# One ring of four PSUM banks, and a retention branch whose value products run a block late, in a two-layer hybrid encoder on one core

## Chip, cores and metric

The kernel runs on one core of a Trainium2 chip. The metric is the device time of one execution in microseconds (us). Three runs of the kernel before took 2946.37, 2948.24 and 2952.17 us, a median of 2948.24 us.

## What is computed

A trunk of two layers over 528 tokens (16 learned ones and 512 of the input) of width 1024, in float32. Each layer mixes tokens in two parallel branches, merges them, and adds a feed-forward block. Cut to its core:

```
proj = rms_norm(h) @ w_in
(qkv, z, a, b, q_b, k_b, v_b, g_b, gate_a, gate_b) = split(proj)
# branch a: 8 heads of 128, both directions, 64-token chunks
q, k, v = silu(short_conv(qkv)); q, k l2-normalised
o_a = gated_delta(q, k, v) + flip(gated_delta(flip(q, k, v)))
y_a = (rms(o_a) * gain * silu(z)) @ w_up_a
# branch b: 4 heads, keys of 256, values of 512
o_b = sum_m gamma^|n-m| (rope(q_n) . rope(k_m)) v_m     # both directions
y_b = (rms(o_b) * silu(g_b)) @ w_up_b
h = h + (sigmoid(gate_a) * y_a + sigmoid(gate_b) * y_b) @ w_out
h = h + (silu(x @ w_gate) * (x @ w_up)) @ w_ffn_out      # x = rms_norm(h)
```

After two layers there is a last norm, and the 512 input tokens are written out.

## The kernel before

**Projections.** Activations lie transposed, as eight tiles of 128 features by 528 tokens, each split into a rounded part and a remainder (`xh`, `xl`). A weight block of 1024 x 128 arrives by DMA as `wraw`; ACT rounds it to `whi` and DVE takes the remainder `wlo` (`split`, lines 178 to 180). `project` then issues three matmuls for each of eight blocks and each half of the tokens (264 columns, or 512 in one piece in the second layer, which drops the learned tokens from most results): 48 or 24 matmuls to an output tile `mmps`, which ACT or DVE reads out of PSUM (`consume`).

**PSUM.** Its eight banks are three rings of [128 x 512] tiles: `pmm` (2 banks) holds the `mmps` of every projection, `pmx` (2, through `pt`) everything that retention, the norms, the sums and the output turns make, and `pmc` (4, through `ct`) the delta rule and the first units behind a norm. A matmul into a ring's next tile waits until the tile that held the bank has been read.

**Mixing.** Four groups of two delta-rule heads run one after the other. `gdn_begin` makes a group's q, k, v, and `gdn_chain` runs its chain: products (`kk`, `kq`), a solve of 32 x 32 blocks on DVE (`st`, `w0`), which goes through DRAM at its start (`nd`, back as `w0`) and its end (`xd`, back as `qc`), the levels that join the blocks (`gdn_levels`: PE `lvy`, `lvt`, `lvq`, `l64`, `l64b`, with DVE and ACT between them), and a scan of five steps (`gdn_scan`: `ks`, `yy`, `sn`, `oo`). It has little PE work and many hand-overs. So `weave` runs it against a filler: each generator yields numbers, its estimated work, and `weave` takes from the filler `NB` = 86 for each `NA` = 71 of the chain. The filler is `filling()`: retention of heads 0 to 2, z gates and merge gates. What is left when the four chains end, and retention of head 3, follows. A scheduler in the framework makes the final order on each engine out of the program's order and priorities.

**Retention** (`retention`, lines 929 to 1017). A mask `strip` is loaded and exponentiated on ACT; q and k are projected, copied by ACT (`rp`, line 946) and rotated on DVE (`rot`). Then, for five chunks, scores `rs` = k.q on PE, times the mask on DVE (`pr`), split into `prh` and `prl`. Then, for four value blocks `dv`, in this order: value projection, ACT copy `rvc` (line 987), turn on PE (`rvt`, `rvm`, lines 995 and 998), split `rv`, gate projection (`rg`), and the weighted sum `rpv` = scores x values. Its yields are 1.8 a chunk, 5.4 a projection and 4.5 a value block.

**After mixing** come the up-projections (`load_a`, `load_b`, results `mrg` and `yb`), the output projection and the feed-forward block. In the last one `done` squares and scales each output half tile and `laid` turns it on PE (`ops`, line 1290) to token order.

Of the kernel before, what the change touches and what calls it, by code (L numbers as in the profile page):

```python
# [48 lines left out]
UB = 6  # L49
TB = 4  # L50

# [46 lines left out]
def trunk(ctx: ExitStack, tc: tile.TileContext, x, meta, norm_mix, w_in, conv_w, a_log, dt_bias, gdn_norm,  # L98
# [6 lines left out]
    tp = ctx.enter_context(tc.tile_pool(name="tp", bufs=TB))  # L105
    pmm = ctx.enter_context(tc.tile_pool(name="pmm", bufs=2, space=PSUM))
    pmx = ctx.enter_context(tc.tile_pool(name="pmx", bufs=2, space=PSUM))
    pmc = ctx.enter_context(tc.tile_pool(name="pmc", bufs=4, space=PSUM))
# [25 lines left out]
    def pt(name="px"):  # L134
        return pmx.tile([P, 512], F32, name=name, tag="mx")

# [165 lines left out]
    with tc.tile_pool(name="ip", bufs=1) as ip:  # L302
# [23 lines left out]
        def turned(i):  # L326
            return pmm.tile([P, 512], F32, name="lay", tag="mm") if i % 2 else pt("lay")

# [72 lines left out]
def layer(tc, nc, env, l, xn, gd):  # L401
# [14 lines left out]
    def acc(tiles):  # L416
        return lambda k: tiles[k]

    def project(src, c0, nt, xs, halves, consume, kts=(8,)):

        xh, xl = xs
        for t in range(nt):
            pss = [pmm.tile([P, 512], F32, name="mmps", tag="mm") for _ in halves]
            k0 = 0
            for j, kt in enumerate(kts):
                w = weights(src[k0 * P:(k0 + kt) * P], c0 + t * P, kt)
                for (n0, n), ps in zip(halves, pss):
                    mm3(ps, w, acc(xh), acc(xl), kt, n0, n, first=j == 0, last=j == len(kts) - 1, k0=k0)
                k0 += kt
            for (n0, n), ps in zip(halves, pss):  # L430
                consume(t, n0, n, ps[:, :n])
# [498 lines left out]
    def retention(h, filler):  # L930
# [32 lines left out]
        pr = []  # L963
        for c in range(NCH):
            m0, m = tok(c)
# [12 lines left out]
            else:  # L978
                split(pst[0:NM, t0:L], pst[32:32 + NM, t0:L], o[0:NM, t0:L])
                nc.scalar.copy(pst[64:64 + NM, t0:L], pst[0:NM, t0:L].bitcast(F32))  # L980
            yield 1.8
        sqa = rp.tile([P, SW], F32, name="rsq", tag="strip")[:, 0:L]
        for dv in range(4):
            vc = tmp("rvc")

            def consume(t, n0, n, ps):
                nc.scalar.copy(vc[:, n0:n0 + n], ps)
            yield from units(W, C_VB + h * DV + dv * P, 1, xn, FULL, consume)
            rv = rp.tile([P, 2, NC * P], F32R, name="rv", tag="rot", bufs=2)
            vh, vl = rv[:, 0], rv[:, 1]  # L990
# [9 lines left out]
            nc.scalar.copy(vst[32:32 + NM], vst[0:NM].bitcast(F32))  # L1000
            gs = tmp("rg")
            yield from units(W, C_GB + h * DV + dv * P, 1, xn, tail, gated(gs))
            o = tmp("ro")
            sq = sqa if dv == 0 else tmp("rsq2")
            for n0, n in tail:
# [5 lines left out]
                act(sq[:, n0:n0 + n], ps[:, :n], AF.Square)  # L1011
                tt(o[:, n0:n0 + n], ps[:, :n], gs[:, n0:n0 + n], MUL)
            nc.sync.dma_start(od_b[h * 4 + dv, :, t0:L], o[:, t0:L])
            if dv:
                tt(sqa[:, t0:L], sqa[:, t0:L], sq[:, t0:L], ADD)
            yield 4.5
        sq = [rp.tile([P, L], F32R, name=n, tag=n, bufs=4) for n in ("prh", "prl")]
        split(sq[0][:, t0:L], sq[1][:, t0:L], sqa[:, t0:L])
        later.append(lambda ps: mean_square(H + h, sq, 4.0 / DV, 4 * 256 * EPS, tmp("ms"), ps))
# [57 lines left out]
    sums(pt)  # L1077
    mixctx.close()

    bctx = ExitStack()  # L1080
# [187 lines left out]
    def done(i, h, n0, n):  # L1268
# [8 lines left out]
        if i == 7 and n0 > NM:  # L1277
            laid(i, h, n0, n)
            finish(n0, n)
        elif i < 7:  # L1280
            laid(i, h, n0, n)
        else:
            half.append((i, h, n0, n))

# [51 lines left out]
```

## Time and profile before

| | before |
|---|---|
| median of three runs | 2948.24 us |
| the profiled execution, its own time | 2948.52 us |
| its span in the trace | 2946.7 us |
| busy: PE, PE weight loads, DVE, ACT | 96%, 87%, 61%, 37% |
| chain that ended last: PE, DVE, DMA, ACT | 80%, 10%, 6%, 3% |
| granted TensorE clock, mean | 0.99 |

PE is the bound, so the time is PE's work and what PE waits. Waits of PE are listed by the line that waited and the instruction whose end released it. The granted clock is a share of full speed: 1.00 is 2.4 GHz, 0.5 is 1.2 GHz. Matmuls are pipelined, so the time of one is read as a chain's piece divided by its count, not from the duration of a single record.

### The profile page before, as it was taken

Reading aid. Unit: us, or ns where it says so; the run is one execution under the profiler, and the core shown is the slowest. Engines: PE = TensorE matmul, PEld = TensorE weight load, DVE = VectorE, ACT = ScalarE, POOL = GpSimd, SP = SyncE. Lnnn points to the kernel's source line nnn. Section 1 sums busy time; section 2 is a strip of 40 time slices with the busy share of each in tenths; the row PEclk is TensorE's granted clock in tenths of the full one; section 3 lists DMA queues with packets and bytes.
Section 4 is the critical chain, followed back from the end, with each engine's and each line's share of the span. In section 5 each row is a group of like instructions: output and inputs, shape, how many; then the busy total and the mean of one; then the engine's idle time right before and its main releaser. Section 6 shows DMA issues by size and latency. Waiting matters only on the chain.

```text
span 2946.7 us, 48876 instructions
## 1 busy us (share of the span) xinstructions
PE 2831.8 (96%) x19487; PEld 2574.8 (87%) x19487; DVE 1802.9 (61%) x3854; ACT 1103.0 (37%) x2171; POOL 9.0 (0%) x114
## 2 busy tenths in 40 slices
PE   8999999999989999999999899999999999999998
PEld 8899998899979999999998797887888778888887
DVE  6867968778565445433358768687785654543333
ACT  5434444344333233222244343443444332332222
POOL 0000000000000000000000000000000000000000
PEclk9999999999999999999999999999999999999999
DMA  6322323234345442333444323334243464433332
GB/s 165 104 80 77 105 77 105 73 78 118 87 147 167 128 142 84 89 93 95 120 116 109 103 68 96 87 83 108 70 118 94 144 188 121 127 108 98 94 107 81
DMA packets 506423, 313.49 MB, mean 106 GB/s; under 512 B 55632, under 2 KB 460778, under 8 KB 506194
## 3 DMA queue, kind: packets, MB, share of 16 engines
q1 hardware_dynamic: 506194, 310.36, 37.1%
q8 instruction: 153, 2.51, 0.4%
q14 instruction: 76, 0.62, 0.1%
HBM read 265.28 MB, written 45.02 MB: 105 GB/s over the span
## 4 chain that ended last, share of the span: by engine, by line
PE 80%; DVE 10%; DMA 6%; ACT 3%; issue 1%; SPq 1%; DVEq 0%; ACTq 0%
PE mmps L113 64%; PE rpv L113 3%; PE oo L113 2%; PE fu L113 1%; DVE wlo L180 1%; PE rs L113 1%; PE sn L113 1%; PE yy L113 1%; DMA lo<-od_a 1%; ACT whi L179 1%; PE ks L113 1%; DMA xd<-w 1%; DVE N L116 1%; DMA gcr<-grow 1%; DMA nd<-NT 1%
## 5 line engine op out<-in xcount | busy, mean ns | idle before, releaser
L113 PE MATMUL mmps<-xh,whi 128*128 128x264 f32 (+1 forms) x3840 | 1195.8, 312 | 24.2 <-ACT rp L946 12.3
L113 PE MATMUL mmps<-xl,whi 128*128 128x264 f32 (+1 forms) x3840 | 1184.9, 309 | 0.0
L113 PE MATMUL mmps<-xh,wlo 128*128 128x264 f32 (+1 forms) x3808 | 1178.6, 310 | 0.5 <-DVE wlo L180 0.5
L113 PEld LDWEIGHTS mmps<-xh,whi 128*128 128x128 f32 x3840 | 730.0, 190 | 69.2 <-ACT rp L946 13.6
L113 PEld LDWEIGHTS mmps<-xl,whi 128*128 128x128 f32 x3840 | 729.3, 190 | 38.3 <-issue 4.0
L113 PEld LDWEIGHTS mmps<-xh,wlo 128*128 128x128 f32 x3808 | 722.6, 190 | 36.8 <-issue 2.3
L180 DVE TENSOR_TENSOR wlo<-wraw,whi 128x1024 fp32r<-128x1024 f32 (+1 forms) x392 | 474.4, 1211 | 457.4 <-ACT whi L179 455.1
L179 ACT CAST whi<-wraw 128x1024 fp32r<-128x1024 f32 (+1 forms) x392 | 408.3, 1042 | 888.9 <-PE mmps L113 667.6
L113 PE MATMUL mmps<-oh,whi 128*128 128x264 f32 (+2 forms) x1126 | 359.2, 319 | 7.2 <-DVE mrg L116 7.0
L113 PE MATMUL mmps<-ol,whi 128*128 128x264 f32 (+2 forms) x1126 | 358.4, 318 | 0.0
L113 PE MATMUL mmps<-oh,wlo 128*128 128x264 f32 (+2 forms) x1126 | 358.0, 318 | 0.0
L113 PEld LDWEIGHTS mmps<-oh,whi 128*128 128x128 f32 x1126 | 211.7, 188 | 24.1 <-DVE mrg L116 5.5
L113 PEld LDWEIGHTS mmps<-oh,wlo 128*128 128x128 f32 x1126 | 211.9, 188 | 15.7
L113 PEld LDWEIGHTS mmps<-ol,whi 128*128 128x128 f32 x1126 | 211.7, 188 | 15.2
L116 DVE SCALAR_TENSOR_TENSOR ac<-xc,cw,ac 128x528 f32<-128x528 f32 x192 | 146.4, 763 | 6.9 <-ACT ac L126 1.4
L119 DVE TENSOR_TENSOR ff<-fg,mmps 128x264 f32<-128x264 f32 (+1 forms) x63 | 32.4, 515 | 115.7 <-PE mmps L113 115.7
L113 PE MATMUL rpv<-prh,rv 128*128 128x264 f32 (+1 forms) x384 | 96.0, 324 | 1.7 <-DVE rv L180 1.7
L113 PE MATMUL rs<-rot 128*128 128x264 f32 (+3 forms) x240 | 82.2, 475 | 11.5 <-DVE pr L119 8.7
L119 DVE TENSOR_TENSOR st<-w 68x30 f32<-68x30 f32 (+14 forms) x240 | 78.2, 326 | 23.1 <-DMA w<-ndm 10.3
L126 ACT ACTIVATE gth<-mmps 128x264 f32<-128x264 f32 (+1 forms) x132 | 60.0, 454 | 61.1 <-PE mmps L113 61.0
L119 DVE TENSOR_TENSOR w<-w,st 68x30 f32<-68x30 f32 (+14 forms) x240 | 78.1, 326 | 6.7
L116 DVE SCALAR_TENSOR_TENSOR hn<-mmps,hold 128x264 f32<-128x264 f32 (+2 forms) x51 | 25.3, 498 | 76.9 <-PE mmps L113 70.9
(315 smaller groups left out, 3191.6 us busy)
## 6 DMA issues: line engine op xcount, KB each, us to landing
wraw<-in_w_in_dram SPq DMA_DIRECT2D x194, 512.0 KB
wraw<-in_w_ffn_in_dram SPq DMA_DIRECT2D x88, 512.0 KB
wraw<-in_w_up_b_dram SPq DMA_DIRECT2D x32, 512.0 KB
wraw<-in_w_ffn_out_dram SPq DMA_DIRECT2D x32, 512.0 KB
gcr<-grow SPq DMA_DIRECT2D x32, 264.0 KB
wraw<-in_w_up_a_dram SPq DMA_DIRECT2D x16, 512.0 KB
wraw<-in_w_out_dram SPq DMA_DIRECT2D x16, 512.0 KB
wraw<-in_w_ffn_out_dram SPq DMA_DIRECT2D x16, 384.0 KB
```

The source lines that it names most:

```text
L113: newest[0] = nc.tensor.matmul(o, lhsT=l, rhs=r, start=start, stop=stop)
L116: (eng or nc.vector).scalar_tensor_tensor(out=o, in0=a, scalar=s, in1=b, op0=op0, op1=op1)
L119: (eng or nc.vector).tensor_tensor(out=o, in0=a, in1=b, op=op)
L126: nc.scalar.activation(o, a, f, **kw)
L179: a = nc.scalar.copy(hi, src)
L180: return a.ins, nc.vector.tensor_tensor(out=lo, in0=src, in1=hi.bitcast(F32), op=SUB).ins
```

## The change

- `pmx` is gone and `pmm` has four banks: projections and all that came through `pt` share one ring.
- After mixing a counter `wide` makes every other projection take its tiles from the delta rule's four banks.
- The body of `retention` is cut into `scores`, `values`, `gates`, `turn` and `weighted`. The first value projection follows the second score chunk, the first gate projection the fourth. Then each round is: the next value projection, the weighted sum of the block before, the turn of the new values, their gate projection. A round's own yield is 3.2 in place of 4.5.
- The output turn of each half tile waits until the next half tile has come.
- The pool of temporaries has 6 buffers (4 before), and the DMA scratch ring is halved.

```diff
-    pmm = ctx.enter_context(tc.tile_pool(name="pmm", bufs=2, space=PSUM))
-    pmx = ctx.enter_context(tc.tile_pool(name="pmx", bufs=2, space=PSUM))
+    pmm = ctx.enter_context(tc.tile_pool(name="pmm", bufs=4, space=PSUM))
...
     def pt(name="px"):
-        return pmx.tile([P, 512], F32, name=name, tag="mx")
+        return pmm.tile([P, 512], F32, name=name, tag="mm")
...
         for t in range(nt):
-            pss = [pmm.tile([P, 512], F32, name="mmps", tag="mm") for _ in halves]
+            wide[0] += wide[0] > 0
+            pss = [(ct if wide[0] % 2 else pt)("mmps") for _ in halves]
...
-        for c in range(NCH):
+
+        def scores(c):
...
-            yield 1.8
-        sqa = rp.tile([P, SW], F32, name="rsq", tag="strip")[:, 0:L]
-        for dv in range(4):
-            vc = tmp("rvc")
+        V, G, S = {}, {}, []
+
+        def values(dv):
+            V[dv] = tmp("rvc")
 
             def consume(t, n0, n, ps):
-                nc.scalar.copy(vc[:, n0:n0 + n], ps)
+                nc.scalar.copy(V[dv][:, n0:n0 + n], ps)
             yield from units(W, C_VB + h * DV + dv * P, 1, xn, FULL, consume)
+
+        def gates(dv):
+            G[dv] = tmp("rg")
+            yield from units(W, C_GB + h * DV + dv * P, 1, xn, tail, gated(G[dv]))
+
+        def turn(dv):
+
+            vc = V[dv]
...
-            gs = tmp("rg")
-            yield from units(W, C_GB + h * DV + dv * P, 1, xn, tail, gated(gs))
+            V[dv] = vh, vl, vst
+
+        def weighted(dv):
+            vh, vl, vst = V[dv]
...
-            yield 4.5
+        for c in range(NCH):
+            scores(c)
+            yield 1.8
+            if c == 1:
+                yield from values(0)
+            if c == 3:
+                yield from gates(0)
+        turn(0)
+        for dv in range(1, 5):
+            if dv < 4:
+                yield from values(dv)
+            weighted(dv - 1)
+            yield 3.2
+            if dv < 4:
+                turn(dv)
+                yield from gates(dv)
...
     mixctx.close()
+    wide[0] = 1
...
-        elif i < 7:
-            laid(i, h, n0, n)
-        else:
-            half.append((i, h, n0, n))
+            return
+        while half:
+            laid(*half.pop())
+        half.append((i, h, n0, n))
```

Since the order is made by a scheduler, three places show it. Every engine has the same number of instructions as before. The first place is PE in the first retention head of layer 0 (`rs` are the scores, two rows to a chunk, `rvt` the turn of the first value block; between them stand matmuls of projections, cut at the dots). Before:

```order
L113 MATMUL rs_1796<-rot_1405,rot_1613 128x264
L113 MATMUL rs_1800<-rot_1405,rot_1613 128x264
...
L113 MATMUL rs_1821<-rot_1405,rot_1613 128x264 x2
L113 MATMUL rs_1825<-rot_1405,rot_1613 128x264 x2
...
L113 MATMUL rs_1840<-rot_1405,rot_1613 128x264 x2
...
L113 MATMUL rs_1844<-rot_1405,rot_1613 128x264 x2
L113 MATMUL rs_1865<-rot_1405,rot_1613 128x264 x2
L113 MATMUL rs_1869<-rot_1405,rot_1613 128x264 x2
L113 MATMUL rs_1884<-rot_1405,rot_1613 16x264 x2
L113 MATMUL rs_1888<-rot_1405,rot_1613 16x264 x2
L995 MATMUL rvt_1988<-c_ident_78,rvc_1908 128x128
...
L995 MATMUL rvt_1988<-c_ident_78,rvc_1908 128x128 x3
```

Now:

```order
L112 MATMUL rs_1793<-rot_1402,rot_1610 128x264 x2
L112 MATMUL rs_1797<-rot_1402,rot_1610 128x264 x2
L112 MATMUL rs_1818<-rot_1402,rot_1610 128x264 x2
...
L112 MATMUL rs_1822<-rot_1402,rot_1610 128x264 x2
L112 MATMUL mmps_1837<-xh_97,whi_1841 128x264
...
L112 MATMUL rs_1926<-rot_1402,rot_1610 128x264 x2
L112 MATMUL rs_1930<-rot_1402,rot_1610 128x264 x2
L112 MATMUL rs_1945<-rot_1402,rot_1610 128x264 x2
L112 MATMUL rs_1949<-rot_1402,rot_1610 128x264 x2
L112 MATMUL mmps_1964<-xh_97,whi_1968 128x264
...
L112 MATMUL rs_2035<-rot_1402,rot_1610 16x264 x2
L112 MATMUL rs_2039<-rot_1402,rot_1610 16x264 x2
L1008 MATMUL rvt_2078<-c_ident_75,rvc_1836 128x128 x4
```

The scores of two chunks now stand together, with a whole projection behind each pair (`mmps_1837` and its second half, then `mmps_1964` and its second half), and all four turns of the first value block stand behind the second of these projections, where one of them stood right behind the last scores.

The second place is DVE at the end of the third group's solve in layer 0: `qd` and `qe` are the turns of the solved blocks and wait for their DMA `qc`; `pr` reads the scores out of PSUM. Before:

```order
L119 TENSOR_TENSOR w0_5337<-w0_5337,st_6723 68x30
L119 TENSOR_TENSOR pr_7109<-rs_7114,strip_6457 128x264
L180 TENSOR_TENSOR prl_7119<-pr_7109,prh_7118 128x528
L119 TENSOR_TENSOR pr_7144<-rs_7145,strip_6457 128x264
L683 STREAM_TRANSPOSE qd_6790<-qc_6787 32x128 x2
L683 STREAM_TRANSPOSE qe_6791<-qc_6787 64x128
L683 STREAM_TRANSPOSE qe_6791<-qc_6787 128x128
L119 TENSOR_TENSOR pr_7144<-rs_7149,strip_6457 128x264
L180 TENSOR_TENSOR wlo_7781<-wraw_7778,whi_7780 128x1024
L683 STREAM_TRANSPOSE qd_6790<-qc_6787 32x128 x2
L119 TENSOR_TENSOR TT_6805<-qe_6791,c_bm2_514 128x256
L119 TENSOR_TENSOR pr_7172<-rs_7173,strip_6457 16x264
```

Now:

```order
L118 TENSOR_TENSOR w0_5469<-w0_5469,st_6924 68x30
L179 TENSOR_TENSOR wlo_7972<-wraw_7969,whi_7971 128x1024
L115 SCALAR_TENSOR_TENSOR rg_7494<-gth_7554,mmps_7496 128x264
L686 STREAM_TRANSPOSE qd_6960<-qc_6944 32x128 x2
L686 STREAM_TRANSPOSE qe_6961<-qc_6944 64x128
L686 STREAM_TRANSPOSE qe_6961<-qc_6944 128x128
L686 STREAM_TRANSPOSE qd_6960<-qc_6944 32x128 x2
L118 TENSOR_TENSOR TT_6975<-qe_6961,c_bm2_511 128x256
L118 TENSOR_TENSOR QT_6971<-qd_6960,c_bm_509 128x512
L118 TENSOR_TENSOR QT2_6972<-qd_6960,c_bm_509 128x512
L179 TENSOR_TENSOR wlo_8041<-wraw_8038,whi_8040 128x1024
```

In the old order scores `pr` of two chunks stood behind `qd`. In the new one retention is further on by then, the scores stand ahead of the solve's end, and only weight remainders `wlo` stand behind `qd`.

The third place is PE in the levels of layer 0's fourth group. Before (second head):

```order
L113 MATMUL lvt_9434<-Y_9372,QT2_9352 128x128 x4
L113 MATMUL lvq_9435<-QT2_9352,Y_9372 128x128 x4
L113 MATMUL mmps_10106<-xh_104,whi_10110 128x264
...
L113 MATMUL l64_9451<-TT_9355,N_8550 64x64 x4
L113 MATMUL mmps_10107<-xh_101,whi_10110 128x264
...
L113 MATMUL l64_9457<-TT_9355,N_8550 64x64 x4
L113 MATMUL mmps_10107<-xh_103,whi_10110 128x264
...
L113 MATMUL l64b_9463<-Qf_9353,Y2_9450 64x64 x4
L113 MATMUL mmps_10107<-xh_106,whi_10110 128x264
...
L113 MATMUL l64b_9469<-Qb_9354,Y2_9450 64x64 x4
```

Now (first head, up to the second head's `l64b`):

```order
L112 MATMUL lvt_9468<-Y_9466,QT2_9386 128x128 x4
L112 MATMUL lvq_9469<-QT2_9386,Y_9466 128x128 x4
L112 MATMUL l64_9485<-TT_9389,N_8601 64x64 x4
L112 MATMUL l64_9491<-TT_9389,N_8601 64x64 x4
L112 MATMUL l64b_9557<-Qf_9387,Y2_9484 64x64 x4
L112 MATMUL l64b_9563<-Qb_9388,Y2_9484 64x64 x4
L112 MATMUL lvy_9604<-QT_9588,N_8777 128x128 x4
L112 MATMUL lvt_9611<-Y_9609,QT2_9589 128x128 x4
L112 MATMUL lvq_9612<-QT2_9589,Y_9609 128x128 x4
L112 MATMUL l64_9629<-TT_9592,N_8777 64x64 x4
L112 MATMUL l64_9635<-TT_9592,N_8777 64x64 x4
L112 MATMUL l64b_9641<-Qf_9590,Y2_9628 64x64 x4
```

There were projection matmuls between each two steps. Now none stands from the first head's `lvt` to the end of the scan, 100 rows further on; in the old order the first scan step and most of the second had them too. The same holds in layer 1. Retention of head 3 has its q and k projections ahead of these levels now.

## Rows read from the trace of the kernel before

**Rows 1.** The page, first line and part 1: span, busy time of each engine.
```profile
span 2946.7 us, 48876 instructions
PE 2831.8 (96%) x19487; PEld 2574.8 (87%) x19487; DVE 1802.9 (61%) x3854; ACT 1103.0 (37%) x2171; POOL 9.0 (0%) x114
```

**Rows 2.** Waits of PE: line waited for, releaser: us in total, times, longest.
```profile
PE mmps L113 <- ACT rp L946: 12.3, 6, 4.8
PE rs L113 <- DVE pr L119: 8.7, 6, 3.5
PE lvy L113 <- DVE QT L119: 8.1, 5, 3.5
PE rvt L995 <- ACT rvc L987: 7.1, 6, 1.7
PE mmps L113 <- DVE mrg L116: 7.0, 3, 2.4
PE mmps L113 <- ACT xc L538: 6.8, 9, 1.5
PE mmps L113 <- DVE rg L116: 3.5, 4, 1.7
PE rvt L995 <- DVE w L119: 3.1, 1, 3.1
PE oms L113 <- ACT prh L179: 2.7, 1, 2.7
```

**Rows 3.** Timeline of ACT, 505 to 524 us: start, us, operation, idle before.
```profile
517.14 0.98 ACT L126 ACTIVATE strip<-strip 128x928 f32<-128x928 f32 x1 [9.41 <-DVE strip L116]
518.02 0.36 ACT L946 COPY rp<-mmps 128x264 f32<-128x264 f32 x1
```

**Rows 4.** Timeline of DVE, 552 to 562 us, the same columns.
```profile
560.10 0.61 DVE L683 STREAM_TRANSPOSE qd<-qc 32x128 f32<-32x128 f32 x2 [3.73 <-DMA qc<-xd]
...
561.17 0.39 DVE L119 TENSOR_TENSOR pr<-rs,strip 128x264 f32<-128x264 f32 x1
```

**Rows 5.** Windows: length, busy PE, PEld, DVE, ACT, POOL, then PEclk, DMA, GB/s.
```profile
147.50:154.50 7.00, 6.10 (x29) 6.06 (x30) 4.33 (x15) 1.85 (x3) 0.38 (x5) 0.51 0.26 71
516.00:523.20 7.20, 4.76 (x22) 4.76 (x23) 6.72 (x20) 2.47 (x4) 0.00 (x0) 0.53 0.00 0
560.50:567.50 7.00, 5.89 (x22) 4.45 (x23) 6.28 (x14) 4.61 (x15) 0.00 (x0) 0.51 0.31 75
1693.80:1700.70 6.90, 5.66 (x26) 5.70 (x27) 5.07 (x9) 2.11 (x6) 0.00 (x0) 0.51 0.15 43
1806.40:1813.40 7.00, 6.10 (x28) 6.10 (x29) 5.94 (x15) 2.45 (x5) 0.38 (x5) 0.51 0.13 15
800.00:820.00 20.00, 18.22 (x142) 16.26 (x141) 15.04 (x50) 6.25 (x20) 0.00 (x0) 1.00 0.11 27
```

**Rows 6.** Chain that ended last, a long piece: start, us, what.
```profile
977.32 87.85 PE mmps L113 x718
```

**Rows 7.** The same chain, 205 to 216 us, first delta-rule group.
```profile
208.06 0.62 PE l64b L113 x11
...
210.91 1.13 PE lvy L113 x8
```

**Rows 8.** The same chain, 797 to 825 us, scan of the fourth group.
```profile
805.96 0.89 PE ks L113 x8
...
807.16 0.38 ACT xx L126
...
807.56 0.36 DVE xx L123
...
810.94 0.94 PE ks L113 x8
```

**Rows 9.** The same chain, 745 to 775 us, levels of the fourth group.
```profile
752.57 3.70 PE mmps L113 x28
...
769.44 0.89 PE lvy L113 x8
```

More of the change, by code (lines that the diff above doesn't have):

```diff
@@ L49 @@
 UB = 6
-TB = 4
+TB = 6
 TCKW = dict(schedule_with_timeline_sim=True)
@@ L326, in turned @@
         def turned(i):
-            return pmm.tile([P, 512], F32, name="lay", tag="mm") if i % 2 else pt("lay")
+            return pt("lay")
         def lay(src, i, part, ps):
@@ L417, in acc @@
         return lambda k: tiles[k]
+    wide = [0]
     def project(src, c0, nt, xs, halves, consume, kts=(8,)):
@@ L1000, in retention @@
             nc.scalar.copy(vst[32:32 + NM], vst[0:NM].bitcast(F32))
-            gs = tmp("rg")
-            yield from units(W, C_GB + h * DV + dv * P, 1, xn, tail, gated(gs))
+            V[dv] = vh, vl, vst
+        def weighted(dv):
+            vh, vl, vst = V[dv]
             o = tmp("ro")
-            sq = sqa if dv == 0 else tmp("rsq2")
+            sq = tmp("rsq2") if S else rp.tile([P, SW], F32, name="rsq", tag="strip")[:, 0:L]
+            S.append(sq)
             for n0, n in tail:
@@ L1011, in retention @@
                 act(sq[:, n0:n0 + n], ps[:, :n], AF.Square)
-                tt(o[:, n0:n0 + n], ps[:, :n], gs[:, n0:n0 + n], MUL)
+                tt(o[:, n0:n0 + n], ps[:, :n], G[dv][:, n0:n0 + n], MUL)
             nc.sync.dma_start(od_b[h * 4 + dv, :, t0:L], o[:, t0:L])
             if dv:
-                tt(sqa[:, t0:L], sqa[:, t0:L], sq[:, t0:L], ADD)
-            yield 4.5
+                tt(S[0][:, t0:L], S[0][:, t0:L], sq[:, t0:L], ADD)
+        for c in range(NCH):
[14 more added lines that the diff above has]
+                yield from gates(dv)
         sq = [rp.tile([P, L], F32R, name=n, tag=n, bufs=4) for n in ("prh", "prl")]
-        split(sq[0][:, t0:L], sq[1][:, t0:L], sqa[:, t0:L])
+        split(sq[0][:, t0:L], sq[1][:, t0:L], S[0][:, t0:L])
         later.append(lambda ps: mean_square(H + h, sq, 4.0 / DV, 4 * 256 * EPS, tmp("ms"), ps))
@@ L1323 @@
     from concourse.bass_utils import run_bass_kernel_spmd as run
-    nc = bacc.Bacc("TRN2", target_bir_lowering=False, num_devices=1, dynamic_dma_scratch_size=2048)
+    nc = bacc.Bacc("TRN2", target_bir_lowering=False, num_devices=1, dynamic_dma_scratch_size=1024)
     arrays, args = {}, []
```

## The prediction

> **What bounds the kernel now.** I read the page first: PE is busy 2831.8 of 2946.7 us [rows 1], so at most some 115 us are there to be had by order alone, since PE keeps every matmul. The reader is to see that no other engine comes near its span.
>
> The waits of PE say where those 115 us lie [rows 2]. Most are in the mixing stage: projections wait for ACT to copy a tile of the ring of two (`rp`, 12.3 us, longest 4.8) or for DVE (`rg`, 3.5); scores wait for `pr` (8.7); turns of values wait for `rvc` (7.1) or for DVE's solve (`w`, 3.1); levels wait for `QT` (8.1). `mrg` (7.0) is behind mixing.
>
> Then the queues of the engines that were waited for. ACT does the longest `rp` copy only after `strip`, for which it had sat idle 9.41 us: copy and mask stand in one queue, and two banks cover one projection [rows 3]. DVE has the same: it waits 3.73 us for `qc`, and reads a score tile (`pr`) only behind the turns [rows 4].
>
> Then the windows behind these gaps [rows 5]. In each the granted clock is 0.51 to 0.53, that is 1.2 GHz, for about 7 us, though PE is busy there: the idle time is paid a second time. PE's price per matmul is from the chain: 87.85 / 718 = 0.122 us for 264 columns at full clock [rows 6].
>
> **What goes.** The sum is against the profiled execution, 2948.52 us, 0.3 over the median of three.
>
> 1. The ring of four. `rp` and `rg`, 15.8 us together [rows 2]: four banks let PE run one more projection ahead, two halves of 24 matmuls at 0.122, 5.9 us, more than the longest wait of 4.8. I take 14.5. The `mrg` waits fall for the same reason and by `wide`: 6 of 7.0.
> 2. Scores spread among projections. In the order now a whole projection stands behind each pair of chunks, 48 x 0.122 = 5.9 us, and the scores stand ahead of the turns for which DVE waits. Of 8.7 us I take 8.
> 3. Values a block late. The turn stands behind a further projection, where `rvc` has been copied and DVE's wait for the first solve is not in its way: 9.5 of 7.1 + 3.1.
> 4. `oms` for `prh`, 2.7 in one wait: the sum over scores now stands later; 2.5.
> 5. `lvy` for `QT`, 8.1 in five waits. The longest two followed a chain with nothing between: one shows 208.06 + 0.62 to 210.91, 2.2 us [rows 7]. The new order has projections there in the first three groups; the last group's stays. I take 5.
> 6. The clock. Five windows behind these gaps hold 4.76 + 5.89 + 5.66 + 6.10 + 6.10 = 28.5 us of PE's busy time at half clock [rows 5]. At full clock it would take half, so 14.3 goes with the gaps; I take 13.
>
> Together 14.5 + 6 + 8 + 9.5 + 2.5 + 5 + 13 = 58.5 us. The rest stays: `xc` (6.8) waits for copies that ACT's new order still has behind the squares of the group before. Output turns show no wait that a later place would mend: nothing. More temporaries and a smaller scratch ring: nothing, no row has PE waiting for either; if the DMA ring were too small, it would be weight blocks late, as `wlo` waits.
>
> **What comes.** Retention's rounds yield 3.2 for 4.5, so `weave` spends the filler faster, and in the last group of each layer it is used up. Before, the levels from the first head's `lvt` to the second head's `lvy` had projections between: the chain piece from 752.57 to 769.44 starts with 28 of them [rows 9]. Now nothing is there, and PE waits for each hand-over. The long one of this kind that a row shows is 2.2 us for `l64b` to `lvy` [rows 7]. The short ones are like that in a scan step without filler, where the chain leaves PE from the copy at 807.16 to the end of the one at 807.56 + 0.36, 0.8 us; such a step takes 810.94 - 805.96 = 4.98 us [rows 8]. In a layer there are one change of heads at 2.2, six other hand-overs between 0.8 and 2.2, and two or three more bare scan steps at 0.8. The low end is 2.2 + 4.8 + 2 = 9, the high end 2.2 + 13.2 + 2 = 17.4. The short ones are single copies of parts of a tile, nearer to the scan step than to the chain of four DVE operations in 2.2; I take 10. Two layers: 20 us, with ends of 18 and 35. Behind such gaps I expect one window at half clock a layer, which costs half of some 5 us busy, as in [rows 5]: 5 us.
>
> 2948.5 - 58.5 + 20 + 5 = 2915 us. Moves that I cost at nothing: value products behind a block (their place is covered by the projection ahead of them) and the tiles that projections take from the delta rule's ring after mixing, when it is nearly empty; without that cover each costs a copy.
>
> **The rivals.**
>
> *The new bare stretch is cheap.* If PE's queue hides the short hand-overs, the 25 us don't come: 2890. For it speaks that PE was 91% busy in 800 to 820 us with little filler [rows 5]; against it, that each level needs the one before.
>
> *The ring brings nothing.* ACT's copies may come late whatever the ring is, since `strip` holds ACT for 9.41 us and not 5 [rows 3]. Then `rp`, `rg` and `mrg` stay, 20.5 us, and two of the windows with (4.76 + 6.10) / 2 = 5.4: 2915 + 26 = 2941. Against it: PE waited 4.8 of those 9.41, and two more banks hold 5.9 us of work. The Trainium skill, "TensorE: Matmul & The Clock Gate", section "HAM oscillation — how this bites in real kernels", reports of a matmul kernel that double-buffering in PSUM gave no further gain. By that rule the time is this rival's. The trace before can't settle it, since it has only rings of two.
>
> *The waits change their name.* DVE and ACT run in order, and what the scheduler puts behind a DMA waits. If half of the 58.5 us comes back so, at other lines, and the 25 us come: 2948.5 - 29 + 25 = 2944, no difference that can be told. For it: the `xc` waits, which no ring mends; against: the order shows no score behind `qc` in the third group.
>
> *Slower: the bare stretch at half clock.* Levels and scan without filler are some 34 us a layer (five steps of 5, levels of 9, an estimate), PE busy for 34 x 18.22 / 20.00 = 31 [rows 5, 8]. If its idle shares keep the clock at 1.2 GHz throughout, 31 us more come in each layer, less some 10 of hand-overs that then hide: 2915 + 62 - 10 = 2967. It decides from the point where 39 of those 62 us are at half clock. Against it: 800 to 820 us, three bare scan steps, ran at 1.00 [rows 5].
>
> **How the numbers follow.** The forecast has a chance of 0.58, the cheap stretch 0.12, the ring without gain 0.10, renamed waits 0.11, half clock 0.09. A measurement of this kernel tells a change from none at about 0.2%, 5.9 us. Faster by more: 0.58 + 0.12 + 0.10 = 0.80. Within: 0.11. Slower: 0.09. The forecast's own bounds are 2913 and 2930 from the hand-overs, and some 15 more either way if the gains of 1 to 6 are a quarter off. The range takes in the cheap stretch and the renamed waits, 2886 to 2948, and leaves out the half clock.
>
> **What would show it.** Right: `rp`, `rg`, `rs` and `rvt` nearly gone from the waits of PE, no window at half clock near the strips' exponentials, and new waits of `lvt`, `l64`, `l64b`, `lvy` and `yy` in the fourth groups alone, 20 us together. The steps are wrong if `rp` waits stay as long (ring), if `pr` and `rvc` are named again behind DMAs (order), if the fourth groups show no waits, or if the granted clock is near 0.5 over the whole scan.

## The result, and the profile after

The changed kernel takes 2921.26 us, the median of four runs (2919.60 to 2922.58), against 2948.01 us (2946.37 to 2952.17) for the kernel before beside it: a ratio of 0.9906 [0.9890, 0.9922], 26.8 us faster. The forecast was 2915 us, 33.5 us faster. The profiled execution is the one of 2919.60 us. Three lines of its page, against [rows 1] and the shares of the chain told there:

```profile
span 2917.7 us, 48775 instructions
...
PE 2822.1 (97%) x19487; PEld 2579.0 (88%) x19487; DVE 1795.2 (62%) x3854; ACT 1101.0 (38%) x2171; POOL 9.0 (0%) x114
...
PE 84%; DVE 8%; DMA 5%; ACT 2%; issue 1%; SPq 0%; DVEq 0%; ACTq 0%
```

The span fell by 29.0 us. Time in which PE does not work, span less busy, fell from 114.9 to 95.6 us, so 19.3 of the 29.0 are waits. PE's busy time fell by 9.7 with the same 19487 matmuls. The waits of PE after, as in [rows 2]:

```profile
PE lvy L112 <- DVE QT L118: 21.4, 6, 10.4
PE mmps L112 <- DVE rg L115: 12.4, 8, 4.2
...
PE mmps L112 <- ACT xc L541: 5.3, 5, 1.5
PE nps L112 <- DVE nacc L118: 4.2, 5, 1.2
PE mmps L112 <- DVE ro L118: 4.0, 2, 3.3
PE rs L112 <- DVE z L115: 2.4, 2, 1.3
PE lvt L112 <- DVE Y L118: 2.3, 3, 0.8
PE yy L112 <- DVE r L115: 1.9, 6, 0.5
```

No line is left for `rp`, for `rs` behind `pr`, for `mrg`, or for `oms` behind `prh`; of `rvt` behind `rvc` and `w` nothing is left either. Those were 12.3 + 8.7 + 7.0 + 2.7 + 7.1 + 3.1 = 40.9 us [rows 2]. In their place stand `lvy` with 13.3 us more than before, `rg` with 8.9 more, and `ro`, `nps` and `z`, and 2.1 us for `pr` at `mmps` and `rvm`.

The longest wait now is at the place where the forecast put the bare stretch, the levels of layer 1's fourth group. The timeline of PE there, 2214 to 2232 us (start, us, operation, idle before):

```profile
2215.39 2.08 PE L112 MATMUL lvy<-QT,N 128*128 128x128 f32 x8 [10.42 <-DVE QT L118]
...
2227.93 2.08 PE L112 MATMUL lvy<-QT,N 128*128 128x128 f32 x8 [3.04 <-DVE QT L118]
```

What PE waits for stands in the chain that ended last, 2190 to 2230 us:

```profile
2200.99 1.24 DVE rot L118 x2
...
2202.62 6.12 DMA xd<-w
...
2209.17 2.13 DMA qc<-xd
...
2213.07 1.33 DVE rot L118 x2
2214.40 0.33 DVE TT L118
2214.74 0.61 DVE QT L118
```

The solve ends on DVE at 2202.6; its way through DRAM (`xd`, `qc`) takes until 2211.3, and PE has no filler left for it. Two rotation steps of retention's head 3 also stand in the way, between `qc` and `QT`. The timeline of DVE in that solve, 2163 to 2176 us, shows what stretched it:

```profile
2165.95 1.23 DVE L179 TENSOR_TENSOR wlo<-wraw,whi 128x1024 fp32r<-128x1024 f32 x1 [0.44 <-ACT whi L178]
2167.09 0.29 DVE L118 TENSOR_TENSOR w<-w,st 68x130 f32<-68x130 f32 x1
...
2171.50 1.23 DVE L179 TENSOR_TENSOR wlo<-wraw,whi 128x1024 fp32r<-128x1024 f32 x1 [0.74 <-ACT whi L178]
2172.64 0.37 DVE L118 TENSOR_TENSOR w<-w,st 68x210 f32<-68x210 f32 x1
```

DVE works in order: a step of the solve that is ready waits behind a weight remainder `wlo` that itself waits for ACT. Seven remainders, six of which waited for ACT (3.9 us together), eight rotation steps and five steps of the mask lie among its own steps, so that this solve takes from 2163.0 to 2202.5, 39.5 us. The first and the last step of the same solve in the kernel before, from its timeline of DVE, 2160 to 2230 us:

```profile
2181.81 0.20 DVE L119 TENSOR_TENSOR st<-w 68x30 f32<-68x30 f32 x1 [3.78 <-DMA w<-ndm]
...
2213.59 0.19 DVE L119 TENSOR_TENSOR w<-w,st 68x30 f32<-68x30 f32 x1
```

It took 32.0 us, with five remainders, one of which waited (0.9 us), and eight other steps among its own. It ended later than now, at 2213.8, but PE still had filler then and did not wait for this `lvy` at all. So PE stands now because the filler is spent, and the stretched solve makes the stand longer.

Last, the clock. Windows of the changed kernel, the five places of [rows 5] (the program is up to some 12 us earlier or later there now), and the fourth groups of both layers from 772 and from 2210 us (columns as in [rows 5]):

```profile
516.00:523.20 7.20, 7.20 (x61) 7.05 (x61) 7.20 (x13) 2.45 (x6) 0.00 (x0) 1.00 0.70 189
772.00:782.00 10.00, 6.18 (x32) 5.55 (x30) 4.73 (x12) 2.92 (x10) 0.00 (x0) 0.54 0.14 43
785.00:795.00 10.00, 10.00 (x52) 8.99 (x51) 5.93 (x19) 3.89 (x13) 0.00 (x0) 0.66 0.01 2
812.00:822.00 10.00, 7.76 (x41) 6.84 (x42) 2.10 (x4) 2.98 (x9) 0.00 (x0) 0.66 0.08 28
...
2210.00:2223.00 13.00, 6.82 (x37) 6.31 (x38) 5.72 (x14) 3.85 (x13) 0.00 (x0) 0.50 0.30 59
2227.00:2233.00 6.00, 4.29 (x18) 4.00 (x19) 2.17 (x4) 0.73 (x4) 0.00 (x0) 0.50 0.00 0
...
147.50:154.50 7.00, 5.85 (x48) 5.85 (x49) 6.60 (x18) 2.58 (x6) 0.00 (x0) 1.00 0.29 78
560.50:567.50 7.00, 7.00 (x60) 6.98 (x59) 5.75 (x19) 2.20 (x6) 0.00 (x0) 1.00 0.39 114
1693.80:1700.70 6.90, 6.90 (x54) 5.97 (x54) 5.86 (x10) 4.23 (x8) 0.13 (x2) 1.00 0.01 2
1806.40:1813.40 7.00, 7.00 (x29) 4.69 (x28) 6.72 (x18) 2.37 (x4) 0.00 (x0) 1.00 0.27 75
```

The five windows at half clock are gone; a shorter stretch, 578 to 582 us, has come behind the `lvy` of the third group. Five new windows in the fourth groups, at 0.50 to 0.66, lose, by busy time times what is missing to 1.00, 2.8 + 3.4 + 2.6 + 3.4 + 2.1 = 14.3 us, as much as the five lost before. Both kernels have more such stretches elsewhere, for instance one of the kernel before and one of the changed kernel:

```profile
822.00:830.00 8.00, 5.95 (x22) 3.86 (x23) 2.04 (x3) 2.61 (x9) 0.00 (x0) 0.59 0.15 52
```

```profile
380.00:388.00 8.00, 6.51 (x33) 6.51 (x34) 5.22 (x12) 3.64 (x12) 0.00 (x0) 0.57 0.32 99
```

Read so in steps of 2 us over the whole execution, the loss to the clock is 22.9 us before and 28.1 us after. The mean granted clock did not rise either: 0.990 before, 0.987 now. (This mean counts idle time too; the loss does not.)

### The profile page after: what moved, and what is told of

It is laid out like the page before. It is cut to its first block, busy times and chain, and to the rows that moved or that the text cites. A ratio compares the mean times of both kernels' runs of the same rounds, so it can differ in the third digit from the quotient of the medians.

```text
span 2917.7 us, 48775 instructions
## 1 busy us (share of the span) xinstructions
PE 2822.1 (97%) x19487; PEld 2579.0 (88%) x19487; DVE 1795.2 (62%) x3854; ACT 1101.0 (38%) x2171; POOL 9.0 (0%) x114
## 4 chain that ended last, share of the span: by engine, by line
PE 84%; DVE 8%; DMA 5%; ACT 2%; issue 1%; SPq 0%; DVEq 0%; ACTq 0%
PE mmps L112 67%; PE rpv L112 3%; PE fu L112 2%; PE oo L112 2%; PE sn L112 1%; DVE wlo L179 1%; PE yy L112 1%; DMA xd<-w 1%; PE ks L112 1%; DMA lo<-od_a 1%; PE rs L112 1%; PE lvy L112 1%; PE lvt L112 1%; DMA lo<-od_b 1%; PE lvq L112 1%
## 5 line engine op out<-in xcount | busy, mean ns | idle before, releaser
L112 PE MATMUL mmps<-xh,whi 128*128 128x264 f32 (+1 forms) x3840 | 1188.0, 310 | 23.7 <-DVE rg L115 12.4
L112 PEld LDWEIGHTS mmps<-ol,whi 128*128 128x128 f32 x1126 | 211.6, 188 | 16.4 <-DVE ol L179 0.9
L112 PE MATMUL rs<-rot 128*128 128x264 f32 (+3 forms) x240 | 75.1, 456 | 2.8 <-DVE z L115 2.4
```

The lines of the kernel that those rows point to most:

```text
L112: newest[0] = nc.tensor.matmul(o, lhsT=l, rhs=r, start=start, stop=stop)
```

## The experiments

The two theories with which they began: the time went because the ring let PE run ahead of ACT's and DVE's copies, and what stops PE now is the bare stretch in the fourth groups; or the ring alone gives nothing and the order of retention gives the gain. Ratios are to the kernel before, measured beside each. It took 2948.01 to 2951.68 us in these places, and the changed kernel was not measured again beside the others, so that a difference to it in us can be some 3 us off.

### The ring alone

The kernel before with nothing but the ring:

```diff
-    pmm = ctx.enter_context(tc.tile_pool(name="pmm", bufs=2, space=PSUM))
-    pmx = ctx.enter_context(tc.tile_pool(name="pmx", bufs=2, space=PSUM))
+    pmm = ctx.enter_context(tc.tile_pool(name="pmm", bufs=4, space=PSUM))
...
     def pt(name="px"):
-        return pmx.tile([P, 512], F32, name=name, tag="mx")
+        return pmm.tile([P, 512], F32, name=name, tag="mm")
```

> The kernel before with one change: one ring of four banks in place of two rings of two. Theory (the ring is worth its own waits): the rp and rg waits of PE, 15.8 us before, shrink to under 3, the mrg waits (7.0) to under 3, and the half-clock windows near 518 and 1807 us go (5.4 us), while rs and rvt waits stay near 8 and 10: about 2948 - 25 = 2923 us. Rival (the ring brings nothing, since the copy behind the strip's exponential is late whatever the ring is): rp waits stay at 4 us or more each, about 2948. Second rival (the whole gain is the ring's): 2921.

Measured: 2958.75 us, 1.0024 [1.0014, 1.0034], slower than before, where the theory had 2923 us and the rivals 2948 and 2921. The ring does what the first term says: waits for `rp` fall from 12.3 to 1.3 us, `rg` to 0.6, `mrg` to none. But two lines come that are not in [rows 2] at all:

```profile
PE rpv L112 <- ACT rv L178: 17.6, 12, 2.7
PE ops L1289 <- ACT hn L125: 16.9, 8, 2.2
```

The first is a change of order. In layer 1 the scheduler had put 13 to 26 matmuls of projections between the turn of the values (`rvt`) and the weighted sum that needs it; with one ring there are none in 11 of the 16 places and 2 to 6 in the others. PE's timeline and ACT's, 1640 to 1652 us:

```profile
1647.33 0.49 PE L994 MATMUL rvt<-c_ident,rvc 128*128 128x128 f32 x3
1649.36 0.50 PE L112 MATMUL rpv<-prh,rv 128*128 128x512 f32 x1 [1.53 <-ACT rv L178]
```

```profile
1647.29 1.05 ACT L178 CAST whi<-wraw 128x1024 fp32r<-128x1024 f32 x1 [3.85 <-PE mmps L112]
1648.24 0.59 ACT L125 ACTIVATE gth<-mmps 128x512 f32<-128x512 f32 x1
1648.73 0.57 ACT L178 CAST rv<-rvt 128x512 fp32r<-128x512 f32 x1
```

The turn ends, ACT still has a weight block and a gate ahead of the copy `rv`, and PE stands. The second line is the same with the output turns. From the chain that ended last, 2880 to 2960 us:

```profile
2889.95 1.04 ACT whi L178
2891.00 0.56 ACT fsq L125
2891.58 0.73 ACT hn L125
...
2892.35 0.66 PE ops L1289 x4
```

All of `whi`, `fsq` and `hn` is bare here. PE waits 2.2 us at seven such places and 1.5 at an eighth. Where the two kinds of tiles had rings of their own, a projection was placed ahead of a tile that was not ready; a projection in the same ring would take the bank behind it, and it now stands behind it in PE's order too. That the shared ring makes the order is what the two orders show; which rule of the scheduler does it was not tried.

The same with the late output turns of the change:

```diff
-        elif i < 7:
-            laid(i, h, n0, n)
-        else:
-            half.append((i, h, n0, n))
+            return
+        while half:
+            laid(*half.pop())
+        half.append((i, h, n0, n))
```

> The ring of four alone and the late output turns, nothing else of the change. Theory (turns and ring belong together): the ops waits of 16.9 us in the kernel with the ring alone fall to 1.5, so 2959 - 15 = 2944 us, and rpv waits stay near 20. Rival (what the ring lost is spread over many places): 2955 or more.

Measured: 2936.85 us, 0.9960 [0.9947, 0.9974]. That is 21.9 us less than the ring alone by the medians and some 19 by the ratios; `ops` falls from 16.9 to 1.5 us, `rpv` behind `rv` stays at 17.8. The step that the forecast costed at nothing is worth some 20 us once the ring is shared.

### The change with the ring taken back

Two rings of two as before, all else as changed (without `wide`, which needs the one ring):

```diff
-    pmm = ctx.enter_context(tc.tile_pool(name="pmm", bufs=4, space=PSUM))
+    pmm = ctx.enter_context(tc.tile_pool(name="pmm", bufs=2, space=PSUM))
+    pmx = ctx.enter_context(tc.tile_pool(name="pmx", bufs=2, space=PSUM))
...
-            pss = [(ct if wide[0] % 2 else pt)("mmps") for _ in halves]
+            pss = [pmm.tile([P, 512], F32, name="mmps", tag="mm") for _ in halves]
```

> The changed kernel with the two rings of two back and projections in the first of them always; retention's new order, yields and late output turns stay. Theory: rp, rg and mrg waits come back, some 20 us with their half-clock windows 26, while rs, rvt and rvc waits stay under 4: about 2921 + 26 = 2947 us. Rival (the order of retention carries the gain, the ring nothing): 2921. If ring and order overlap, between: 2930.

Measured: 2938.60 us, 0.9950 [0.9938, 0.9963]. Half of the gain is there without the ring. `rp` shows 2.6 us and not 12.3: retention's order alone takes most of the wait that the forecast gave to the ring. `mrg` stays (8.7), so do the `oms` waits behind `prl` and `prh` (3.1 and 2.6). `rg` waits 0.4 us here, 0.6 with the ring alone and 12.4 with both: those waits need the shared ring and the new order together.

### Without the sharing after mixing

```diff
     mixctx.close()
-    wide[0] = 1
```

> The changed kernel without the alternation of projections between the two rings after mixing; the order of the mixing stage is the same instruction for instruction up to there. Theory (four banks are enough after mixing; the mrg waits were the ring of two): 2921, within 4 us, mrg waits under 2. Rival (the alternation is what took the mrg waits away): mrg waits of 6 to 7 us come back, about 2928.

Measured: 2933.98 us, 0.9944 [0.9931, 0.9956], 12.7 us over the changed kernel: neither the theory's 2921 nor the rival's 2928. There is still no wait for `mrg`; new or longer are `oms` behind `prh` (4.9), `mps` (1.2) and `xps` (1.0), 7.1 together. The loss to the clock, read as above, is 40.7 us against 28.1, and PE's time without work 99.4 us against 95.6, so between the two profiled executions, 13.8 us apart, most is clock. It isn't all chance: the run with the clock 0.986 took 2931.12 us, and the changed kernel's run with 0.986 took 2921.94. Which wait the alternation saves, and whether the lower clock of the other runs comes with it, was not settled.

This kernel and the one with two rings of two have the same order of retention and no `wide`, and differ in the ring (and in which ring the tiles `lay` of the layout come from). They took 2933.98 and 2938.60 us, 0.9944 [0.9931, 0.9956] and 0.9950 [0.9938, 0.9963], no difference that can be told. So the parts don't add up: the ring with late turns gave 0.9960 in the old order, the new order with two rings 0.9950, and both together without `wide` 0.9944. About half of the change's gain is there by either way, and the rest came only with `wide`.

### Values and turns in their old places

In the changed kernel, the weighted sum right behind its own gates:

```diff
         turn(0)
-        for dv in range(1, 5):
-            if dv < 4:
-                yield from values(dv)
-            weighted(dv - 1)
+        weighted(0)
+        yield 3.2
+        for dv in range(1, 4):
+            yield from values(dv)
+            turn(dv)
+            yield from gates(dv)
+            weighted(dv)
             yield 3.2
-            if dv < 4:
-                turn(dv)
-                yield from gates(dv)
```

> The changed kernel with each value block's weighted sum right behind its own gate projection again, as before, while the scores stay spread among projections. Theory (the ring's order puts rpv behind rvt, and only the late sum hides the split rv): rpv waits for rv of some 1.5 us each come back, 12 to 16 of them, 17 to 20 us: 2921 + 18 = 2939. Rival (spreading the scores carries the gain in retention): 2921 to 2925.

Measured: 2931.28 us, 0.9934 [0.9916, 0.9951], 10.0 over the changed kernel, between theory and rival. `rpv` behind `rv` is back (10.3 us in 7 waits by ACT, 1.8 by DVE), as in the ring alone, but `lvy` falls from 21.4 to 8.4, so that PE's time without work is only 4.7 us longer (100.3 against 95.6). The loss to the clock is 7.8 us more (35.9 against 28.1), and the run with the highest clock, 0.988, took 2923.85 us, 4.3 over the changed kernel's run with 0.987. The eight waits for `rg` are there too, at `rpv` instead of `mmps` (14.3): they are there, one a head, wherever the weighted sum stands.

And the output turns in their old place, the diff of the late turns read backwards:

> The changed kernel with the output turns undone: each half tile is turned as soon as it has come. Theory formed after the ring alone (in one ring a tile is taken in the order of the program, so a turn that waits for ACT's hn holds the projections behind it): ops waits of 8 x 2.2 us come back, less the 1.5 that every kernel has, so 2921 + 16 = 2937 us. Rival (the prediction's step that the late turns are worth nothing): 2921.

Measured: 2934.63 us, 0.9955 [0.9938, 0.9971], over four runs from 2924.93 to 2939.88 which go with their granted clock (0.987 and 0.981). At the clock of the changed kernel, 0.987, the cost is 2924.93 - 2919.60 = 5.3 us, not 15, from one run of each: `ops` waits 3.7 instead of 1.5, `whi` 2.8. In the old order and without `wide` the same move was worth some 20; that the projections behind the turn have other banks now may be the reason, and was not tried apart. Why the same kernel got another clock from run to run is open.

### Filling the bare stretch

The old yield, with which the filler lasts longer:

```diff
             weighted(dv - 1)
-            yield 3.2
+            yield 4.5
```

> The changed kernel with one number back: a retention round yields 4.5 as before, not 3.2, so that the filler is spent more slowly. In the order this puts 12 us of filler between the first and the second head's lvy in both last groups, where 2 and 0 stood. Theory (the bare levels cost what the profile of the changed kernel shows there): the lvy wait of 10.4 us at 2215 and those of 3.0 go, with half-clock windows: 20 us or more, about 2900. Rival (filler taken from earlier groups opens waits there, the sum stays): 2921. Rival (the bare scan, which is still bare, is the larger part): 2912.

Measured: 2920.76 us, 0.9894 [0.9881, 0.9908], the same as the changed kernel. The wait of 10.4 us is gone, but `lvy` still waits 16.5 us, now ten times up to 3.4, in every group but the last, and `sn` 5.0: the rival, that filler taken from earlier groups opens waits there.

Retention of head 3 inside the filler:

```diff
         yield from merge_gates(G0 + 3 * GF, 14)
+        yield from retention(3, merge_gates(14, 16))
...
-    for _ in retention(3, merge_gates(14, 16)):
-        pass
```

> The changed kernel with retention of head 3 put at the end of the filler, so that the filler does not run out: the last groups' levels and scan then have projections between them in the order (10 us of them from the first to the second lvy, 25 and 13 us in the scans, where there were 0 to 2). Theory (the bare stretches cost what their gaps and half-clock windows show in the changed kernel, some 25 us): about 2896 to 2900. Rival (the fill only moves the waits, as with the yield of 4.5): 2921. Second rival (retention's own scores and copies then sit in DVE's and ACT's queues among the levels and hold the chain up): slower than 2921.

Measured: 2923.01 us, 0.9907 [0.9892, 0.9922], the same again. Its waits of PE:

```profile
PE mmps L112 <- ACT oh L178: 31.9, 4, 16.3
...
PE lvy L112 <- DVE QT L118: 3.9, 3, 2.6
```

The fourth group is covered, and the wait has moved behind it: the up-projection of branch a waits for its input `oh`, at its longest 14.9 us in layer 0 and 16.3 in layer 1, since nothing is left to cover the end of the chain. The filler is spent either way; where it stands moves the wait and doesn't shorten it.

### The delta rule's chain, shorter and longer

If the chain on DVE sets the end of mixing, a shorter solve must be worth more after the change than before. Both kernels leave out 14 of 30 pairs of steps of the solve (the expectation says 13):

```diff
-            tt(t, bc(w3[:, 0:q, q:q + 1], [68, q, n]), bc(w3[:, q:q + 1, q + 1:32], [68, q, n]), MUL)
-            tt(w3[:, 0:q, q + 1:32], w3[:, 0:q, q + 1:32], t, ADD)
+            if q % 2 or q > 28:
+                tt(t, bc(w3[:, 0:q, q:q + 1], [68, q, n]), bc(w3[:, q:q + 1, q + 1:32], [68, q, n]), MUL)
+                tt(w3[:, 0:q, q + 1:32], w3[:, 0:q, q + 1:32], t, ADD)
```

> The changed kernel that leaves out 13 of the solve's 30 pairs of DVE steps (so the blocks aren't fully inverted), some 8 us less of DVE's chain in each of eight groups; PE's matmuls are all there. Theory (with the ring waits gone the delta-rule chain bounds the mixing stage, and the filler is short of it): lvy waits fall from 21 us to under 8, and the time by 15 to 25 us, to about 2900. Rival (PE's waits are set by the queues and not by the chain's length): 2921, the waits under other names.

> The kernel before, with the same 13 of 30 pairs of solve steps left out. Theory (before, ring and turns bound the mixing stage, the chain had room): at most the lvy waits of 8 us go, 2950 - 5 = 2945, a smaller fall than in the changed kernel. Rival (the chain bound the kernel before as much): the same fall as there, 20 us, 2930.

Measured: on the changed kernel 2901.40 us, 0.9831 [0.9816, 0.9845]; on the kernel before 2940.72 us, 0.9967 [0.9953, 0.9981], where 2951.68 us stood beside both. The same cut is worth 0.0075 (0.9906 to 0.9831) after the change and 0.0033 before, some 22 and 10 us. On the changed kernel:

```profile
PE mmps L112 <- DVE rg L115: 12.4, 8, 3.4
...
PE lvy L112 <- DVE QT L118: 4.8, 3, 2.9
```

`lvy` falls from 21.4 to 4.8 us and the mean clock is 0.990; `rg` does not move. On the kernel before `rp` (12.6), `rs` (9.8) and `rvt` (8.5) stay. So the chain's length counts about twice as much after the change as before, though before it was not free either: 10 us went where at most 5 were expected. The cut shortens the chain and also DVE's work as a whole, by 71 us in both kernels; which of the two counts, these two runs don't separate.

Then DVE relieved in a way that keeps the result, six steps of the rotation (two shown) on POOL, which has 9.0 us of work:

```diff
-            tt(r[:, 0, sl], pre[0][:, sl], cos, MUL)
-            tt(u[:, sl], pre[1][:, sl], sin, MUL)
+            tt(r[:, 0, sl], pre[0][:, sl], cos, MUL, nc.gpsimd)
+            tt(u[:, sl], pre[1][:, sl], sin, MUL, nc.gpsimd)
```

> The changed kernel with the six tensor-tensor steps of each rotation of q and k on the idle POOL in place of DVE: some 4 us less of DVE for each of 16 rotations, none of them in the chain itself. Theory (the chain is long because DVE does other work between its steps): lvy and rg waits fall, about 2905 to 2912. Rival (POOL is slow and what it holds, rot and rp tiles, comes late: scores wait for rot): 2925 or more.

Measured: 2955.82 us, 1.0012 [1.0002, 1.0022], 34.6 us over the changed kernel and 0.12% over the one before. Groups of POOL by line (count, busy us, mean ns, idle before), and one of DVE in the changed kernel (count, ns at least, in the median and at most):

```profile
L118 POOL TENSOR_TENSOR rot<-rot,ru 128x528 f32<-128x528 f32 (+1 forms) x32 | 47.7, 1510 | 0.0
L118 POOL TENSOR_TENSOR rot<-rp,c_cos 128x528 f32<-128x528 f32 (+1 forms) x16 | 30.1, 1884 | 246.6 <-ACT rp L949 246.6
```

```profile
L118 DVE TENSOR_TENSOR rot<-rot,ru x32: 650/690/711, 96.4 to 2213.7; 128x528 f32<-128x528 f32 x24, 128x512 f32<-128x512 f32 x8
```

A step costs more than twice as much there. `lvy` did not fall (24.4), scores wait for `pr` (4.7), projections and scores wait for DVE's `z` (6.6 and 5.7), and the clock is 0.981. Nor was DVE relieved: it is busy 1805.4 us against 1795.2, with 96 steps fewer, because others became longer. Rows from the timelines of POOL and DVE, 2005 to 2016 us:

```profile
2011.88 1.33 POOL L118 TENSOR_TENSOR ru<-rp,c_cos 128x528 f32<-128x528 f32 x1
```

```profile
2012.03 1.25 DVE L118 TENSOR_TENSOR st<-w 68x58 f32<-68x58 f32 x1
```

The same step of the solve took 0.22 us in the changed kernel's solve above (at 2163.49 us). Fifteen steps of the solve take 1.25 to 1.46 us here, each beside a rotation step on POOL, where none took over 0.41 in the changed kernel, and eight of them are in layer 1's fourth group. So the rotation on POOL held up the chain itself, and what a freer DVE would give stays untested.

Last, the chain made longer and the ring deeper, five banks and three:

```diff
-    pmm = ctx.enter_context(tc.tile_pool(name="pmm", bufs=4, space=PSUM))
-    pmc = ctx.enter_context(tc.tile_pool(name="pmc", bufs=4, space=PSUM))
+    pmm = ctx.enter_context(tc.tile_pool(name="pmm", bufs=5, space=PSUM))
+    pmc = ctx.enter_context(tc.tile_pool(name="pmc", bufs=3, space=PSUM))
```

> The changed kernel with five banks in the ring of projections and three for the delta rule. After the change projections wait 12.4 us in 8 waits for DVE to read a tile through rg (longest 4.2), and 4.0 in 2 for ro. Theory, that these waits are banks that DVE has not read yet: one more bank is 24 matmuls of 0.122 us, 2.9 us of work ahead, so that only the two longest waits keep something, 12.4 falls to some 2 to 3 and ro to about 1; the delta rule takes at most four tiles at a time (kk, kq, km of two heads, lvt and lvq), and with three banks its levels and scan wait some 10 to 15 us more on PE for their banks, of which filler hides the greater part in three of four groups. Then 2912 to 2918 us. Rival, that the delta chain sets the end of the mixing stage: rg waits fall too, but what the chain loses with three banks (32 level products and 160 scan products wait for a copy of 0.3 to 0.5 us) comes back at lvy, lvt, yy and sn in full, and the time is 2925 to 2940 us.

Measured: 2958.82 us, 1.0026 [1.0017, 1.0035]. The waits of PE:

```profile
PE lvy L112 <- DVE QT L118: 45.1, 12, 14.0
...
PE mmps L112 <- DVE rg L115: 1.2, 1, 1.2
```

The waits for `rg` go with one more bank, as the theory said: 12.4 to 1.2, and `ro` has no line. The time is worse than even the rival's 2925 to 2940: `lvy` waits 23.7 us more. The first `lvy` of the four groups of layer 1 start at 1680.0, 1873.2, 2067.5 and 2251.1 us, where the changed kernel has 1671.0, 1852.4, 2033.4 and 2215.4, so that the second and the third group come 193 to 194 us behind the one before and not 181. That fits a chain slowed by its three banks, which PE's list of waits shows only in part: PE's time without work is 5.7 us longer (101.3 against 95.6), its busy time 31.4, of which the loss to the clock is 11.5 (39.6 against 28.1). Where the rest lies was not found. So here five banks for projections can't be had at the chain's expense.

No version here that does the whole computation is faster than the changed kernel beyond its interval.

## Why the prediction was right, and where its steps were not

The sign, the size to 6 us, most of the waits that go and the place of the new ones came as forecast. Several steps behind the sum did not, and that the total fits is in part luck. The sum had 45.5 - 20 = 25.5 us of waits and 13 - 5 = 8 us of clock. PE's time without work gave 19.3, the clock cost some 5, and 9.7 us came from PE's busy time, for which the sum had no term but the clock.

1. *The ring (14.5 + 6).* The waits went by the mechanism named, but the sum was wrong. `rp` and `mrg` went, but alone the ring is slower by 0.24%, since one ring also ties the order of projections to that of turns and weighted sums. Half of the gain comes without it, since `rp` goes to 2.6 us by order alone, and in the new order without `wide` the ring adds nothing that can be told (0.9944 against 0.9950). And `rg` did not go: with `ro` it waits 16.4 us, more than `rp` and `rg` together before. "Four banks let PE run one more projection ahead" forgot that the scores, turns and sums now take banks of the same four.
2. *Scores (8).* `pr` went at `rs`, 8.7 us; 2.1 for it elsewhere and 2.4 for `z` came.
3. *Values late (9.5).* 10.2 to nothing. In the shared ring the place also takes the `rpv` waits: undone, they are 12.1 us, `lvy` is 13.0 less, and the median is 10.0 us higher, at a like clock some 4.
4. *`prh` (2.5).* 2.7 to nothing; but `nps` behind `nacc` went from 1.3 to 4.2, a sum over squares that waits at another line.
5. *`lvy` (5 gained) and the bare stretch (20 lost).* Net 15 us more was forecast; `lvy`, `lvt`, `l64b`, `yy` and `sn` together wait 28.1 us after and 15.3 before, 12.8 more. 17.9 of the 21.4 at `lvy` are in the fourth groups. The size was right, the place only in part: the forecast counted hand-overs inside the levels and the scan, at most 2.2 us each, and the longest wait, 10.4, lies ahead of them, where the solve's end goes through DRAM (2202.62 to 2211.30) with no filler left.
6. *The clock (13 gained, 5 lost).* The gain came at the five places named. The loss was forecast as one window a layer, 5 us in all; the fourth groups have five, 14.3 us by the windows above, so that the clock gave back what it brought, and the stretches elsewhere did not become fewer. This is the step that failed in its result: 8 us of net gain were in the sum, and 22.9 us of loss became 28.1. The row that spoke for a cheap clock in the bare scan, 800 to 820 us at 1.00 [rows 5], ends 2 us ahead of a stretch at half clock, 822 to 830 us, in the sums over the chain's output.
7. *Output turns and `wide` (nothing).* Wrong in kind. With the shared ring the late turns are worth 5 to some 20 us, since they take away the turns that it makes projections wait for, and `wide` 9 to 13, for a reason not found. The forecast costed each edit against the kernel before, where no such wait stands; the right reference is the kernel with the ring already in it. The errors of 1 and 7 have opposite signs, which is part of why the sum held.

Of the rivals, *the waits change their name* is true in part: `rg`, `ro`, `nps` and `z` grew by some 18 us. *The ring brings nothing* is true of the time of the ring alone, and of the ring in the new order without `wide`, though not for its reason, since the waits of [rows 3] did go. The Trainium skill, "TensorE: Matmul & The Clock Gate", section "HAM oscillation — how this bites in real kernels", tells of a matmul kernel in which double-buffering in PSUM gave no further gain. The ring alone, 1.0024, and the ring in the new order without `wide`, 0.9944 against 0.9950, agree; the ring with the late turns, 0.9960, does not, unless the turns alone were worth that much, which was not run, and neither does the whole change, 0.9906. *The bare stretch is cheap* and *half clock throughout* both fell: it costs, in stretches.

What the account leaves open: of PE's busy time, 9.7 us less at a clock that was not higher. A matmul's record lasts 0.28 us where the pitch is 0.122, so by an estimate busy time counts some 0.16 more wherever PE breaks off, and it breaks off less often now: its lists of waits have 94 waits before and 66 after, some 4.5 us by this estimate. The rest of the 9.7 is not accounted for.

## What to carry to other kernels

Cost the parts of a change in the surroundings that the other parts make, not one by one against the old trace: a shared ring of PSUM banks removed the waits for a copy here, and made tiles whose input was late hold the tiles behind them, so that it paid only with those tiles moved later, and on top of the new order only with the spare banks of `wide`. So test a part also by taking it out of the whole change, alone and together with the part that it may need. When PE's waits go, look at the chain that ran under them: here filler moved its waits without shortening them, and only a shorter solve, one that leaves steps out, gave time (0.9906 to 0.9831). Idle time that was moved into one long stretch brought its own half clock, so price the new stretch's clock by the same rows as the old one's, and read the rows past the end of the stretch.

## What was not expected of the hardware

The tensor operation of 128 x 528 float32 took 1.5 to 1.9 us on POOL against 0.69 on DVE, and steps of 0.2 to 0.4 us on DVE took 1.25 to 1.46 beside it. The clock followed the shape of the idle time and not only its sum: in the changed kernel 2210 to 2223 and 2227 to 2233 us, with PE busy 6.82 of 13.00 and 4.29 of 6.00 us, ran at 0.50 throughout, while the kernel with the old yield, whose `lvy` waits 16.5 us in ten pieces and whose PE is without work 98.2 us and not 95.6, had a mean of 0.990 and lost 22.0 us to the clock and not 28.1. It was no faster for it (2920.76 and 2921.26 us), and why not is open. In one kernel, the output turns undone, the mean granted clock lay between 0.981 and 0.987 from run to run, and the time differed by 15 us with it.
